# A hybrid streaming encoder step on one core: wider memsets between GpSimd operations, and late attention probabilities scaled by whichever of two engines the planner picks

## The chip, the core and the metric

The kernel runs on one core of a Trainium2 chip. A core has a matrix engine (PE in the profile; its weight loads are listed apart as PEld), a vector engine (DVE), a scalar engine (ACT), a general engine called GpSimd (POOL), and a queue (SP) from which this kernel issues its transfers between the chip's memory and the core's own memory. Each engine works through its instructions in the order in which they were written; semaphores make one engine wait for another.

The metric is the time of one execution in device microseconds. Before the change, three executions took 1264.11, 1261.85 and 1261.01 us, a median of 1261.85 us.

## The reference

One layer of a streaming encoder is computed for a prompt of 2048 frames and a sample of 64 frames, with 1024 features. Half of the mixed features come from an attention of 8 heads by 64 over a band of 576 keys (512 earlier frames and the chunk of 64 that the query is in), the other half from a gated linear recurrence of 4 heads by 128. Both share one input projection from 1024 to 4096 columns.

```python
def mixer_layer(x, ln_g, w_in, lb, norm_g, w_out, attn_fn, s0):
    aq, ak, av, ag, hq, hf, hi, hg = jnp.split(rms_norm(x, ln_g) @ w_in, SPLITS, axis=-1)
    o_a = attn_fn(heads(aq), k, v).reshape(B, T, W_A) * jax.nn.silu(ag)
    o_b, S = hgrn2_branch(hq, hf, hi, hg, lb, norm_g, s0)
    y = x + jnp.concatenate([o_a, o_b], axis=-1) @ w_out
    return y, k, v, S

def band_attention(q, k, v, rel, valid, rel_bias):
    s = jnp.einsum('bnqhd,bnkhd->bnhqk', q, k) * ATTN_SCALE + bias
    s = jnp.where(valid[None, :, None], s, NEG_INF)
    p = jax.nn.softmax(s, axis=-1)
    return jnp.einsum('bnhqk,bnkhd->bnqhd', p, v)
```

A last RMSNorm follows the layer. The outputs are the normalized rows, the newest keys and values, and the states of the recurrence. All inputs are float32.

## The kernel before

**Precision and tiling.** Float32 operands are split into a high and a low part, and a product is made of three matmuls (high by high, low by high, high by low). The prompt is worked in four superblocks of 512 frames; the 64 frames of the sample ride along with the second. For each superblock, 32 projections of 128 columns are made in a fixed list (`JOBS`): for each of four groups, the four parts of the recurrence (`hf`, `hq`, `hi`, `hg`) and the four of the attention (`pg`, `pq`, `pk`, `pv`). As soon as a group is projected, its recurrence or its pair of attention heads is worked beside the projections that follow. The tiles `xh` and `xl` are the two parts of the normalized input, `w` the weights, `acc` the banks of results; in the attention `s` holds scores, `pr` probabilities, `nm` the negated row maxima, `sm` the row sums, `tr` transposed probabilities, `ph` their two parts, `pv` the product with the values, and `mixa` the gated result. In the recurrence, `pf`, `sf`, `fq` and `fk` are small decay factors made on GpSimd from `eb`; with them `q` and `k` are scaled before `g`, `bl`, `asb` and so on are formed.

**What sets the order.** No order is written out by hand. A planner (class `Plan`, line 53) runs a main generator, which issues the projections' matmuls two at a time, and many small generators ("threads") for everything else, and it keeps a clock for every engine. Each operation passes through `Queue.__getattr__`, so nearly all rows of the profile carry its line, 266. There the operation's estimated cost is charged to its engine's clock; a thread that has asked for an engine goes on when the estimated time has come. An estimate that changes therefore changes which thread goes next, and with it the order of the operations from there on, on every engine. `Plan.pick` returns the engine whose clock, plus a cost given with the call, is the lowest.

**The breath.** When three or more GpSimd operations are issued while GpSimd's clock is ahead of the matrix engine's, the planner puts a memset of a small tile, `C.breath`, between them. The planner charges a memset on GpSimd 95 ns and 0.85 ns for each column.

**The softmax.** For 128 query rows of one head, one vector instruction adds the bias to the scores and leaves the row maximum (`pr<-s,bias`, shown as ISA in the order and as CUSTOM_DVE_ANT_0 in the profile); ScalarE takes the exponential and the row sum (`pr<-pr,nm`); VectorE takes the reciprocal of the sum (`RECIPROCAL sm`); then the row is multiplied with it (`pr<-pr,sm`). This last step, in `softmax_exp`, runs on VectorE. It runs on ScalarE once the set `have` contains `"parts"`, which the program adds when the output projection has begun to run beside the attention. That is so only for the last pair of heads of the last superblock: 8 of the 128 x 640 scalings, out of 96.

**The output projection.** `w_out` is split on the chip by the thread `out_weights` during the third superblock and written to memory (`wod<-xn`, 28 transfers); the input rows of the next superblock are loaded to `xn` tiles (`xn<-in_x_prompt_dram`), whose sum of squares (`ck<-xn`) and root (`rstd`) ScalarE computes before VectorE scales them and the matrix engine transposes them (`g<-ident,xn`). Near the end of the program the output projection adds partial sums in `xn<-xn,acc` on VectorE, after ScalarE has copied one of the banks (`asb<-acc`).

Of the kernel before, what the change touches and what calls it, by code (L numbers as in the profile page):

```python
# [8 lines left out]
F32 = mybir.dt.float32  # L9
# [8 lines left out]
P = 128  # L18
D = 1024
# [353 lines left out]
def hymba_step(  # L373
# [24 lines left out]
    C = Plan()  # L398
# [6 lines left out]
    cst = ctx.enter_context(tc.tile_pool(name="cst", bufs=1))  # L405
# [7 lines left out]
    def T(pool_, shape, dt, tag, **kw):  # L413
        uid[0] += 1
        C.name(homes.get(id(pool_), ""), tag, kw.get("bufs") or 1, f"{tag}_{uid[0]}")
        return pool_.tile(list(shape), dt, tag=tag, name=f"{tag}_{uid[0]}", **kw)
# [37 lines left out]
    mask = T(cst, [P, P], U32, "mask")  # L454
    eps_t = T(cst, [P, 1], F32, "eps")
    one_t = T(cst, [P, 1], F32, "one")
    C.breath = T(cst, [P, 1], F32, "breath")
    reset = T(cst, [P, 512], F32, "reset")
    asb = [T(cst, [P, 4, P], F32, f"asb{i}") for i in range(2)]
    g_norm = T(cst, [P, NHB], F32, "gnorm")  # L460
# [5 lines left out]
    have = set()  # L466
# [544 lines left out]
    def softmax_rows(d, h, qc, spans, bcol, nk, out):  # L1011

        yield lambda: d.q_n >= qc + P and d.k_n >= qc + P and d.bias_at is not None
        yield max(d.q_t, d.k_t, d.bias_at) + 300.0
        yield from tk["s_ps"].get()
        yield from tk["pr"].get()
        sps = s_ps()
        for part in (d.q, ql):
            for i, (k0, kn) in enumerate(spans):
                mm(sps[:, i, :kn], part[:, h, qc : qc + P], d.kd[:, h, k0 : k0 + kn], kn,  # L1020
                   start=part is d.q, stop=part is ql)
        t = C.pe()
        yield "D", t
        s = T(wk, [P, 640], F32, "pr", bufs=PRB)
        nm = T(wk, [P, 2], F32, "nm", bufs=4)
        ns, kn = len(spans), spans[0][1]
        dve.tensor_tensor_reduce(
            s[:, :nk].rearrange("p (a c) -> p a c", a=ns), sps[:, :ns, :kn],
            d.bias[:, h, bcol : bcol + nk].rearrange("p (a c) -> p a c", a=ns),
            1.0, 3e38, ALU.add, ALU.min, nm[:, 0:1])  # L1030
        t = C.dve(nk + 80, t)
        tk["s_ps"].put(1, t)
        d.left -= 1
        if d.left == 0:
            if d.sb == len(SUPER) - 1 and d.p == NPAIR - 1:
                have.add("scores")
                tk["x4"].put()
            tk["bias"].put()
        yield "A", t
        yield from softmax_exp(s, nm, nk, out, t)  # L1040

    def softmax_exp(s, nm, nk, out, t):
        sm = T(wk, [P, 1], F32, "sm", bufs=4)
        act.activation(s[:, :nk], s[:, :nk], AF.Exp, bias=nm[:, 0:1], scale=-1.0, accum_out=sm)
        t = C.act(nk + 300, t)
        yield "D", t
        dve.reciprocal(sm, sm)
        t = C.dve()
        if "parts" in have:
            yield "A", t  # L1050
            act.activation(s[:, :nk], s[:, :nk], AF.Copy, scale=sm)
            t = C.act()
        else:
            dve.tensor_scalar(s[:, :nk], s[:, :nk], sm, None, ALU.mult)
            t = C.dve()
        out.append((s, t))
# [184 lines left out]
    def sample_a(d, c0, marks):  # L1241
# [41 lines left out]
        yield "A", t  # L1283
        out = []
        yield from softmax_exp(s, nm, 576, out, t)
        pr, t = out[0]
        yield lambda: marks[-1]["pv"] and turn["ph"] == turn["given"]
# [1008 lines left out]
```

## Time and profile before

| what | value |
|---|---|
| median of three executions | 1261.85 us |
| the profiled execution | 1260.86 us, 0.99 us below that median |
| its span, first to last instruction | 1259.0 us |
| matrix engine busy | 1238.8 us of it (98%) |
| VectorE, ScalarE, GpSimd busy | 891.9, 706.9 and 379.9 us |
| breath memsets | 36, of one column each |
| scalings of 640 columns on VectorE / on ScalarE | 88 / 8 |

A row of a timeline gives the start, the duration, the engine, the operation with what it writes and reads, its size, how many like it stand together, and in brackets how long the engine had been idle and what ended that idle time. Durations overlap, since an engine begins its next instruction before the last one's results are written; a matrix engine that issues at its full pace starts a matmul of 512 columns every 0.23 us (1.40 us for six of them).

### The profile page before, as it was taken

What the parts mean: (1) busy time and instruction counts of PE and PEld (TensorE: products, weight loads), DVE (VectorE), ACT (ScalarE), POOL (GpSimd) and SP (SyncE); (2) the same over time, 40 slices, a digit from 0 to 9 for tenths busy, and PEclk for the clock granted to TensorE, in tenths of its full rate; (3) what the DMA queues carried; (4) which work ended last, traced back from release to release, by engine and by line L of the source; (5) the groups of instructions that cost most, each with busy time, mean ns of one, the idle gap of its engine ahead of it and who ended that gap; (6) DMA issues with size and microseconds to landing.
All of it is one profiled execution on the core that took longest, in us unless ns stands there. A gap on an engine that the chain in (4) does not pass through costs nothing. (4 is left out here: it accounts for less than half of the span.)

```text
span 1259.0 us, 22201 instructions
## 1 busy us (share of the span) xinstructions
PE 1238.8 (98%) x8120; PEld 1081.6 (86%) x8120; DVE 891.9 (71%) x1854; ACT 706.9 (56%) x1548; POOL 379.9 (30%) x703
## 2 busy tenths in 40 slices
PE   9999999999999999999999999999999999999997
PEld 8788887999999999998888888998888888788786
DVE  7786968766857678686584849783838574578886
ACT  6453546665656557575565656764636454753443
POOL 7766655111120210202533634110101104451110
PEclk9999999999999999999999999999999999999999
DMA  7887787645354554636879597646454657886331
GB/s 288 301 288 244 247 282 281 219 168 202 138 188 142 181 200 144 216 125 236 272 248 303 206 364 254 220 164 210 144 212 136 222 178 279 324 277 203 126 134 67
DMA packets 94830, 271.72 MB, mean 216 GB/s; under 512 B 10305, under 2 KB 43073, under 8 KB 77058
## 3 DMA queue, kind: packets, MB, share of 16 engines
q1 hardware_dynamic: 94722, 270.31, 61.4%
q8 instruction: 64, 1.05, 0.3%
q14 instruction: 44, 0.36, 0.1%
HBM read 186.66 MB, written 83.62 MB: 215 GB/s over the span
## 5 line engine op out<-in xcount | busy, mean ns | idle before, releaser
L266 PE MATMUL acc<-xh,w 128*128 128x512 f32 (+2 forms) x2720 | 568.4, 348 | 1.0 <-ACT sig L266 0.8
L266 PEld LDWEIGHTS acc<-xh,w 128*128 128x128 f32 x2720 | 436.7, 189 | 51.7 <-issue 1.4
L266 PE MATMUL acc<-xl,w 128*128 128x512 f32 (+2 forms) x1360 | 297.4, 348 | 0.0
L266 PEld LDWEIGHTS acc<-xl,w 128*128 128x128 f32 x1360 | 219.3, 189 | 24.9 <-issue 0.5
L266 POOL TENSOR_TENSOR mixa<-mixa,sga 128x256 f32<-128x256 f32 (+1 forms) x36 | 29.8, 828 | 334.8 <-DVE mixa L266 259.6
L266 DVE CUSTOM_DVE_ANT_0 pr<-s,bias 128x640 f32<-128x640 f32 (+5 forms) x144 | 100.7, 703 | 34.5 <-PE s L266 33.9
L266 ACT ACTIVATE pr<-pr,nm 128x640 f32<-128x640 f32 (+4 forms) x132 | 100.7, 763 | 39.0 <-DVE nm L266 37.9
L266 ACT CAST ph<-tr 128x512 fp32r<-128x512 f32 (+3 forms) x176 | 88.1, 507 | 59.7 <-PE tr L266 27.9
L266 POOL TENSOR_TENSOR w<-wraw,w 128x256 fp32r<-128x256 f32 x120 | 105.3, 906 | 46.9 <-DVE w L266 25.9
L266 DVE TENSOR_TENSOR ph<-tr,ph 128x512 fp32r<-128x512 f32 (+3 forms) x176 | 101.1, 589 | 10.0 <-ACT ph L266 8.8
L266 PE MATMUL pv<-ph,v 128*128 128x256 f32 (+2 forms) x344 | 97.2, 373 | 3.1 <-DVE ph L266 2.4
L266 PE MATMUL tr<-ident,pr 128*128 128x128 f32 x580 | 91.2, 273 | 2.4 <-DVE pr L266 1.2
L266 PEld LDWEIGHTS tr<-ident,pr 128*128 128x128 f32 x580 | 70.4, 140 | 16.6 <-issue 3.8
L266 ACT ACTIVATE sig<-acc 128x256 f32<-128x256 f32 (+2 forms) x86 | 42.7, 497 | 73.6 <-PE acc L266 73.3
L266 ACT COPY vT<-acc 128x512 f32<-128x512 f32 (+2 forms) x64 | 31.3, 488 | 71.2 <-PE acc L266 71.1
L266 DVE TENSOR_SCALAR pr<-pr,sm 128x640 f32<-128x640 f32 (+3 forms) x124 | 67.9, 547 | 4.4
L266 DVE TENSOR_TENSOR mixa<-mixa,pv 64x256 f32<-64x256 f32 (+1 forms) x144 | 56.8, 394 | 18.9 <-ACT mixa L266 14.7
L266 PEld LDWEIGHTS pv<-ph,v 128*128 128x128 f32 x344 | 57.4, 190 | 10.3 <-issue 2.0
L266 ACT ACTIVATE sig<-sig 128x512 f32<-128x512 f32 (+2 forms) x109 | 57.3, 528 | 10.0 <-DVE gk L266 7.3
L266 PE MATMUL s<-kd,q 128*128 128x320 f32 (+3 forms) x232 | 56.9, 315 | 0.2
L266 POOL TENSOR_TENSOR xn<-wraw,xn 128x256 fp32r<-128x256 f32 x48 | 37.8, 803 | 62.2 <-ACT xn L266 62.1
L266 PE MATMUL s<-kd,ql 128*128 128x320 f32 (+3 forms) x232 | 55.6, 309 | 0.0
(319 smaller groups left out, 2064.5 us busy)
## 6 DMA issues: line engine op xcount, KB each, us to landing
w<-wd SPq DMA_DIRECT2D x96, 1024.0 KB, 5.1
wd<-w SPq DMA_DIRECT2D x32, 1024.0 KB, 7.6
wraw<-in_w_in_dram SPq DMA_DIRECT2D x30, 512.0 KB, 5.5
wod<-xn SPq DMA_DIRECT2D x28, 512.0 KB, 5.0
xn<-in_x_prompt_dram SPq DMA_DIRECT2D x23, 512.0 KB, 5.5
bias<-biasd SPq DMA_DIRECT2D x12, 640.0 KB, 7.5
carry<-kd SPq DMA_DIRECT2D x12, 512.0 KB, 8.0
carry<-v SPq DMA_DIRECT2D x12, 512.0 KB, 5.2
```

The source lines that it names most:

```text
L266: r = f(*args, **kw)
```

## The change

The breath tile has 128 columns rather than one, so each of its memsets writes 128, and the planner charges it 204 ns rather than 96. And a late scaling goes to ScalarE only where the planner's clocks say so: VectorE is chosen if its clock plus 680 ns is not above ScalarE's plus 780 ns (or the current time, or the time at which the reciprocal is done, where these are later than a clock).

```diff
@@ -454,7 +454,7 @@
     eps_t = T(cst, [P, 1], F32, "eps")
     one_t = T(cst, [P, 1], F32, "one")
-    C.breath = T(cst, [P, 1], F32, "breath")
+    C.breath = T(cst, [P, P], F32, "breath")
     reset = T(cst, [P, 512], F32, "reset")
@@ -1046,7 +1046,7 @@
         dve.reciprocal(sm, sm)
         t = C.dve()
-        if "parts" in have:
+        if "parts" in have and C.pick(t, D=680.0, A=780.0) == "A":
             yield "A", t
             act.activation(s[:, :nk], s[:, :nk], AF.Copy, scale=sm)
             t = C.act()
```

In the built program the choice falls on VectorE all 8 times: VectorE has 96 scalings of 640 columns, ScalarE none. There are 35 breaths. Apart from these and a few sums that move between GpSimd and VectorE, the instructions are the same, and their order, with the tiles' running numbers left out, is the same except at four stretches: in the first tens of microseconds, around 715 us, between the third and the fourth superblock (around 764 to 860 us), and in the last pair's attention (around 1069 to 1110 us).

The first place is on the matrix engine, in the first recurrence of the program. `acc` rows are projections, `g<-q,k` the recurrence's small products, `g<-ident,bl` a transpose that needs VectorE's `bl`. Before:

```order
L266 MATMUL acc_600<-xh_156,w_433 128x512 x8
L266 MATMUL acc_600<-xl_157,w_433 128x512 x2
L266 MATMUL g_624<-q_135_518,k_136_519 32x32
...
L266 MATMUL acc_600<-xl_157,w_433 128x512 x6
L266 MATMUL acc_600<-xh_156,w_433 128x512 x2
L266 MATMUL g_672<-ident_69,bl_619 128x128 x4
L266 MATMUL acc_600<-xh_156,w_433 128x512 x6
```

After:

```order
L266 MATMUL acc_596<-xh_156,w_433 128x512 x8
L266 MATMUL acc_596<-xl_157,w_433 128x512 x4
L266 MATMUL g_625<-q_136_526,k_137_527 32x32
...
L266 MATMUL acc_596<-xl_157,w_433 128x512 x4
L266 MATMUL acc_596<-xh_156,w_433 128x512 x6
L266 MATMUL g_676<-ident_69,bl_618 128x128 x4
L266 MATMUL acc_596<-xh_156,w_433 128x512 x2
```

Two more projection matmuls stand ahead of the small products, and four more ahead of the transposes.

The second place is SP's queue of transfers between the third and the fourth superblock. `wod` rows write split output weights, `w` rows load projection weights, `xn` rows load input rows of the fourth superblock, `kd`, `v` and `bias` are for the next pair of heads. Before:

```order
L266 DMA wod_69_141<-xn_9280 256x1x512
L266 DMA wod_73_145<-xn_9279 256x1x512
L266 DMA w_9812<-wd_46_118 128x2048
L266 DMA xn_9836<-in_x_prompt_dram 128x1024
L266 DMA xn_9839<-in_x_prompt_dram 128x1024
L266 DMA mixd_17_89<-mixa_9657 128x256
L266 DMA kd_9905<-carry_3_26_98 128x2x512
L266 DMA v_9906<-carry_3_26_98 128x1024
L266 DMA bias_9910<-biasd_34_106 128x1280
L266 DMA w_9921<-wd_55_127 128x2048
```

After:

```order
L266 DMA wod_69_141<-xn_9303 256x1x512
L266 DMA kd_9833<-carry_3_26_98 128x2x512
L266 DMA v_9834<-carry_3_26_98 128x1024
L266 DMA bias_9838<-biasd_34_106 128x1280
L266 DMA mixd_17_89<-mixa_9653 128x256
L266 DMA wod_73_145<-xn_9302 256x1x512
L266 DMA w_9903<-wd_55_127 128x2048
L266 DMA xn_9940<-in_x_prompt_dram 128x1024
L266 DMA xn_9943<-in_x_prompt_dram 128x1024
L266 DMA w_9955<-wd_51_123 128x2048
```

The two loads of input rows now stand behind the last write of output weights and behind the write of `mixa`, and `kd`, `v` and `bias` stand ahead of both.

The third place is VectorE in the last pair's attention, where the late scalings are. Before:

```order
L266 RECIPROCAL sm_12863<-sm_12863 128x1
L266 ISA pr_12873,nm_12874<-s_12865,bias_12688 128x640
L266 ISA nm_12874 128x1
L266 RECIPROCAL sm_12885<-sm_12885 128x1
L266 ISA pr_12903,nm_12904<-s_12887,bias_12688 128x640
L266 ISA nm_12904 128x1
L266 TENSOR_TENSOR v_12684<-tr_12897,v_12684 128x4x128
L266 COPY sig_12913<-tr_12897 128x512
L266 RECIPROCAL sm_12917<-sm_12917 128x1
L266 ISA pr_12932,nm_12933<-s_12919,bias_12688 128x640
L266 ISA nm_12933 128x1
L266 TENSOR_TENSOR xn_12215<-xn_12215,acc_12880 128x512
```

There the subtractions `ph` (two rows of `ph<-tr,ph`) follow the last of these rows. After:

```order
L266 RECIPROCAL sm_12862<-sm_12862 128x1
L266 TENSOR_SCALAR pr_12855<-pr_12855,sm_12862 128x640
L266 ISA pr_12873,nm_12874<-s_12864,bias_12686 128x640
L266 ISA nm_12874 128x1
L266 RECIPROCAL sm_12896<-sm_12896 128x1
L266 TENSOR_SCALAR pr_12873<-pr_12873,sm_12896 128x640
L266 TENSOR_TENSOR v_12682<-tr_12891,v_12682 128x4x128
L266 COPY sig_12909<-tr_12891 128x512
L266 ISA pr_12919,nm_12920<-s_12898,bias_12686 128x640
L266 ISA nm_12920 128x1
L266 TENSOR_TENSOR ph_12925<-tr_12914,ph_12925 128x512
L266 TENSOR_TENSOR xn_12213<-xn_12213,acc_12879 128x512
```

The scalings stand behind their reciprocals on VectorE, and the first subtraction `ph` stands ahead of the sum `xn<-xn,acc` rather than behind it.

## The prediction

> **What bounds the kernel now.** I read the page's busy times first, then busy time by stretches of the span, then the list of what the matrix engine waits for, then the chain that ended last, and the timeline around each place where the order changes.
>
> ```profile
> PE 1238.8 (98%) x8120; PEld 1081.6 (86%) x8120; DVE 891.9 (71%) x1854; ACT 706.9 (56%) x1548; POOL 379.9 (30%) x703
> ```
>
> The matrix engine (PE) is busy for 1238.8 of 1259.0 us. Neither edit touches the number of projections, so only its 20.2 idle microseconds can shrink, or grow. Where they lie is seen by stretches; the columns are start and end, length, and busy time with the count for PE, its weight loads, VectorE, ScalarE and GpSimd, then the granted clock, the share of the transfer engines and GB/s.
>
> ```profile
> 0.00:80.00 80.00, 75.38 (x471) 63.73 (x472) 60.09 (x112) 41.98 (x89) 55.33 (x92) 1.00 0.83 303
> 760.00:830.00 70.00, 69.39 (x506) 61.14 (x505) 58.75 (x114) 49.67 (x110) 15.27 (x29) 1.00 0.60 215
> 1069.00:1109.00 40.00, 37.63 (x199) 31.35 (x198) 23.20 (x54) 27.91 (x56) 21.32 (x38) 1.00 0.80 293
> 1240.00:1259.00 19.00, 12.44 (x54) 9.73 (x52) 9.56 (x16) 3.80 (x12) 0.00 (x0) 0.92 0.19 72
> ```
>
> Of the 20.2 us, 4.6 lie in the first 80 us, 6.6 in the last 19 us, which the change leaves in order, 0.6 at the boundary between the third and fourth superblock, and 2.4 in the last pair's attention. What can be won is thus 4.6 + 0.6 + 2.4 = 7.6 us at most, 0.6% of the time. The list of waits (engine and instruction, what it waited for, total, times, longest) names the pieces:
>
> ```profile
> PE pv L266 <- DVE ph L266: 2.4, 2, 1.4
> PE g L266 <- POOL one L266: 1.4, 1, 1.4
> PE g L266 <- DVE xl L266: 1.2, 5, 0.4
> PE g L266 <- DVE asb L266: 1.0, 1, 1.0
> PE g L266 <- DVE k L266: 0.8, 2, 0.5
> ```
>
> The two waits for `ph` are in the last pair's attention, those for `asb` and the longest for `k` in the first recurrence. GpSimd is named once, before any breath is written, so breaths reach PE only through VectorE. Of the chain that ended last I show one row: a run of 119 projection matmuls that start together after the last pair's result has gone through memory; before them PE was idle for about 0.2 us, so that an earlier end of the attention moves the rest with it.
>
> ```profile
> 1132.69 27.88 PE acc L266 x119
> ```
>
> **The first recurrence: a gain of 0.7 us.**
>
> ```profile
> 36.88 0.10 POOL L266 MEMSET breath<- 128x1 f32 x1
> 38.66 0.19 POOL L266 COPY fk<-eb 128x4 f32<-128x4 f32 x1
> 39.22 0.79 DVE L266 TENSOR_TENSOR k<-k,fk 128x256 f32<-128x256 f32 x1
> 40.07 1.01 PE L266 MATMUL g<-q,k 128*32 128x64 f32 x52 [0.53 <-DVE k L266]
> 42.51 0.62 PE L266 MATMUL acc<-xh,w 128*128 128x512 f32 x2
> 44.12 0.63 PE L266 MATMUL g<-ident,bl 128*128 128x128 f32 x4 [0.99 <-DVE asb L266]
> ```
>
> GpSimd makes the factors one after another, with three breaths among them; `k<-k,fk` on VectorE waits for the last, and PE for that: 0.53 us. The transposes of `bl` come late too. Two matmuls begun at 42.51 at 0.23 us each would have let them start at 42.97; they started at 44.12, so 1.15 us were lost. The order now puts two more projection matmuls ahead of the small products and four ahead of the transposes, 4 x 0.23 = 0.93 us of work done in time that PE waited. Against it stand two wider memsets ahead of `fk` (the third now follows it). A 128-column memset is in the trace once, beside the group of the breaths (minimum, median, maximum in ns):
>
> ```profile
> 0.80 0.20 POOL masks.py:197 MEMSET ident<- 128x128 f32 x1 [0.29 <-POOLq L2283]
> L266 POOL MEMSET breath<- x36: 88/98/642, 23.0 to 1112.7; 128x1 f32 x36
> ```
>
> Each wider breath costs 0.20 - 0.10 = 0.10 us, two cost 0.2, and since the chain from GpSimd over VectorE to PE has no slack here, they count in full: -0.93 + 0.2 = -0.7 us. The bounds are -1.7 (both waits gone, 0.53 + 1.15) and +0.4 (the memsets lengthen the chain twice over and the next product waits as long as before).
>
> **Breaths elsewhere: 0.2 us lost.** The other 33 cost 33 x 0.10 = 3.3 us of GpSimd, which is busy for 30% of the span. They are hidden by PE's projections, as nothing in PE's list waits on GpSimd there. I take 0.2 us, for the few that stand in a chain to VectorE. The bounds are 0 and 3.3, the latter if all such cover were gone; the low end is the nearer, because PE has under 8 us of waits anywhere outside the tail.
>
> **The boundary to the fourth superblock: 0.5 us lost.**
>
> ```profile
> 788.70 1.06 ACT L266 ACTIVATE ck<-xn 128x1024 bf16<-128x1024 f32 x1
> 790.21 0.20 ACT L266 ACTIVATE rstd<-rstd 128x1 f32<-128x1 f32 x1
> 792.42 0.33 SPq L266 DMA_DIRECT2D mixd<-mixa  x1
> 794.28 3.66 SPq L266 DMA_DIRECT2D w<-wd  x2
> 801.36 0.83 ACT L266 CAST kd<-vT 64x256 fp32r<-64x256 f32 x2
> 803.84 0.37 ACT L266 COPY vT<-acc 128x256 f32<-128x256 f32 x1 [1.64 <-PE acc L266]
> 805.64 0.66 PE L266 MATMUL g<-ident,xn 128*128 128x128 f32 x4 [0.16 <-DVE xl L266]
> 820.39 0.66 PE L266 MATMUL g<-ident,xn 128*128 128x128 f32 x4 [0.38 <-DVE xl L266]
> xn<-in_x_prompt_dram SPq DMA_DIRECT2D x3, 512.0 KB, 5.8
> w<-wd SPq DMA_DIRECT2D x3, 1024.0 KB, 7.6
> ```
>
> Before, the input rows are on their way at 782 us and ScalarE squares them at 788.70, in time of its own. Now their two loads stand in SP's queue behind the write of `mixa` (792.42), the last write of output weights and a weight load. They are issued at about 794 us and land, by 5.8 us and half a megabyte between them, at about 800 and 801.5. On ScalarE their squares and roots, 1.7 us a tile (788.70 to 790.41), now stand between the `kd` casts, which end at 802.2, and the copy of `vT`, which before started at 803.84 after 1.64 us of idle time. Two tiles make 3.4 us, so that copy and the casts of `xh` behind it come at about 805.6, 1.8 us later; PE's own work there is also placed about 0.8 us later (eight more matmuls of 256 columns or scores ahead of the transposes), which leaves it waiting for about 1.0 us. What goes is the waits of the two PE rows, 0.16 + 0.38 = 0.54 us: together +0.5. The bounds are -0.5 (the square of the first tile fits into idle time before the casts) and +6.0 (the rival below).
>
> **The last pair: a gain of 1.4 us.**
>
> ```profile
> 1077.03 2.02 PE L266 MATMUL acc<-w,slot 128*128 128x512 f32 x8
> 1080.02 0.70 PE L266 MATMUL pv<-ph,v 128*128 128x512 f32 x2 [0.96 <-DVE ph L266]
> 1089.58 0.39 PE L266 MATMUL acc<-w,xl 128*128 128x512 f32 x1
> 1091.37 0.48 PE L266 MATMUL pv<-ph,v 128*128 128x256 f32 x2 [1.41 <-DVE ph L266]
> 1078.58 0.69 DVE L266 TENSOR_TENSOR xn<-xn,acc 128x512 f32<-128x512 f32 x1 [1.61 <-ACT asb L266]
> 1090.20 0.69 DVE L266 TENSOR_TENSOR xn<-xn,acc 128x512 f32<-128x512 f32 x1 [2.66 <-ACT asb L266]
> L266 ACT ACTIVATE pr<-pr,sm x8: 813/830/833, 1071.1 to 1100.5; 128x640 f32<-128x640 f32 x8
> L266 DVE TENSOR_SCALAR pr<-pr,sm x124: 286/553/1035, 66.7 to 1037.4; 128x640 f32<-128x640 f32 x88, 128x128 f32<-128x128 f32 x8, 128x256 f32<-128x256 f32 x8, 128x384 f32<-128x384 f32 x8
> ```
>
> Eight matmuls from 1077.03 end their turn at 1078.90, and `pv` started at 1080.02: 1.12 us late. The second `pv` could have started at 1089.81 and started at 1091.37: 1.56 late. Both times VectorE held the subtraction that makes `ph` behind a sum `xn<-xn,acc`, which waited for ScalarE's copy `asb` for 1.61 and 2.66 us; and ScalarE was late because scalings of 0.83 us stood ahead of its casts and copies. Now ScalarE loses 8 x 0.83 = 6.6 us, and the first `ph` stands ahead of the sum, so both waits, 2.68 us, can go. VectorE takes on 8 x 0.553 = 4.4 us in a stretch where it is busy for 23.2 of 40, which leaves room on the whole. But it works in order: each scaling stands ahead of the next instruction that reads scores, or of a `ph`. Going through the new order by hand with the rows' durations, I find six of the eight covered by idle time, and two not: one score bank comes free about 0.4 us late, and one later `ph` about 0.8 us. So -2.68 + 1.2, about -1.4 us. The bounds are -2.9 (no new wait, and the 0.2 before the 119 matmuls go too) and +2.3 (as long a wait for `ph` as before, and the lengthening worked out in the rival below).
>
> **The sum.** -0.7 + 0.2 + 0.5 - 1.4 = -1.4 us. The profiled execution took 1260.86 us, 0.99 below the median of the three, so it would take 1259.5; on the median of 1261.85 I forecast 1260.4 us.
>
> **The rivals.** *All named waits go.* Nothing takes the place of the waits at the redrawn places: 0.53 + 1.15 + 0.54 + 2.68 = 4.9 us, or 1257.0 us. For it speaks that the planner draws the order from its clocks anew and that the new order mends exactly the places that wait. Against it speaks that a work order redrawn at four places seldom leaves no wait behind.
>
> *The input rows come late (slower).* Both loads stand behind a weight load, and the row at 794.28 shows two weight loads held until 797.94, because their tiles were in use. If the first of them waits so long, the input rows are issued 3.7 us later, at about 798; and at the 7.6 us of the stretch's weight loads rather than 5.8, they land 1.8 us later still. ScalarE then stands at their squares with the casts of `xh` behind it, and PE, which needs `xh`, waits as long: 5.5 us more than in the sum, 1265.9 us. It decides once the second tile lands after about 802.5 us, when ScalarE would otherwise reach it. Against it: the hold probably belongs to the second of the two weight loads, which stays behind the input rows.
>
> *VectorE and GpSimd get in each other's way.* The scaling takes 553 ns in the middle and up to 1035, and the long ones stand beside GpSimd's work:
>
> ```profile
> 767.68 1.02 DVE L266 TENSOR_SCALAR pr<-pr,sm 128x640 f32<-128x640 f32 x1
> 1081.99 1.43 POOL L266 TENSOR_TENSOR slot<-sig,slot 128x256 fp32r<-128x256 f32 x2 [18.03 <-ACT slot L266]
> ```
>
> GpSimd idles for 18 us up to 1081.99, so the first scalings run free; about five come after it, and 5 x (1.02 - 0.55) = 2.3 us are added to VectorE there. With half of the other breaths' 3.3 us uncovered as well, the sum becomes -1.4 + 2.3 + 1.7 = +2.6, or 1264.5 us, and over 1265.6 if the waits for `ph` stay. The Trainium skill, "SBUF — State Buffer", section "Who interferes with whom", speaks against the change in the same way: a `tensor_scalar` in its two-port mode and GpSimd lock each other out for a whole instruction, while ScalarE never waits on anyone; the two lengths of the scaling agree with it, and by it the sum would be that of this rival. The same section says that a vector instruction with two inputs in SBUF contends with GpSimd instructions that read SBUF and not with one that only writes it; by it a memset of 0.20 us would be a wider opening for VectorE, which no row of before shows, and the 0.2 us lost to breaths would become a small gain.
>
> *The new condition never picks VectorE* has no chance: the order has all eight scalings there.
>
> **How the numbers follow.** About 0.3% (3.8 us) is what a measurement of this kernel can tell from no change. The sum has a chance of 0.42; its own range, 1258 to 1263, lies within that. All waits gone has 0.27, faster. The late input rows have 0.18, slower. The two engines in each other's way have 0.13, of which 0.06 over 0.3% slower. That makes faster 0.27, same 0.49, slower 0.24. The range runs from 1256.0, a microsecond under the second case, to 1266.5, just over the third; beyond it lie 0.1 on each side.
>
> **What would show it.** In the profile after, the 1.0 and 0.5 us that PE waits for `asb` and `k` early should shrink; the waits of `pv` for `ph` near 1080 and 1091 should be gone, with `xn<-xn,acc` behind `ph`; scalings on VectorE in that stretch should take 0.55 to 1.0 us; and near 805 PE should wait for `xh` or `xl` about 1 us. The prediction is wrong if PE's idle time there is several microseconds (input rows after 803 us), if `pv` still waits over a microsecond for `ph`, or if a wait appears in a stretch whose order did not change.

## The result and the profile after

The changed kernel takes 1254.63 us (median; 1253.5 to 1255.5), the kernel before beside it 1261.53 us. The ratio is 0.9942, with a 95% interval of 0.9929 to 0.9955: 0.58% faster, some 7 us. The prediction was 1260.4 us with a range from 1256.0 to 1266.5, so the time lies below the range.

The page's first lines after (busy time, share of the span and instructions):

```profile
span 1252.0 us, 22191 instructions
PE 1234.3 (99%) x8120; PEld 1081.3 (86%) x8120; DVE 893.8 (71%) x1865; ACT 701.4 (56%) x1540; POOL 376.3 (30%) x696
```

The span is 7.0 us shorter, but PE's idle time fell only from 20.2 to 17.7 us. The other 4.5 us came out of its *busy* time, with the same 8120 matmuls. A sum over idle time alone could not have found them. The stretches after, to be held against those of before:

```profile
0.00:80.00 80.00, 76.27 (x477) 64.48 (x478) 62.99 (x115) 43.54 (x92) 56.35 (x92) 1.00 0.83 304
760.00:830.00 70.00, 70.00 (x518) 63.52 (x517) 55.39 (x110) 49.65 (x112) 21.09 (x38) 1.00 0.63 214
1069.00:1109.00 40.00, 39.51 (x209) 33.27 (x208) 30.15 (x68) 23.17 (x52) 24.00 (x40) 1.00 0.94 337
```

PE is busier in all three. To see where the span was saved, I matched the matmuls of the two traces one by one and took the difference of their start times (after less before) at eight marks; what a stretch won or lost is the difference between its two ends. The other columns do the same for three of the kernels below.

| stretch of before, us | after | breath of 128 columns alone | choice of engine alone | unused tile alone |
|---|---|---|---|---|
| 0 to 65 | -1.4 | -1.5 | +1.1 | 0.0 |
| 65 to 238 | +0.4 | +0.4 | +2.5 | +1.2 |
| 238 to 630 | +0.2 | +0.1 | +0.3 | +0.1 |
| 630 to 748 | +1.0 | +0.8 | +0.4 | -0.1 |
| 748 to 890 | -2.1 | -2.2 | 0.0 | -0.1 |
| 890 to 1062 | +0.1 | +0.1 | 0.0 | +0.1 |
| 1062 to 1118 | -2.5 | +0.3 | -1.6 | -0.1 |
| 1118 to the end | -2.6 | -1.9 | -0.3 | -1.9 |
| sum | -6.9 | -3.9 | +2.4 | -0.7 |

Such a column compares one execution with one. In the first 240 us kernels with the same order differ by more than 2 us among themselves, so the sums are not the kernels' times, which are medians of several executions. From 240 us up to the last pair, kernels of the same order agree within 0.5 us in every stretch, and there the columns can be read; in the last two stretches they differ by up to 1.1 us, in the last pair because of one scaling on VectorE that comes up below.

Of the four stretches that won over a microsecond, three had a term in the forecast, which missed in size or, at the boundary, in sign; the last, 2.6 us in the output projection at the end, was not forecast at all. Most of it is a change of *pace*, the time from the start of one matmul to the start of the next. The chain of waits has there, in both kernels, an unbroken run of 180 matmuls of 512 columns (start, duration, engine, tile). Before, and then after:

```profile
1210.68 41.77 PE acc L266 x180
```

```profile
1204.52 40.93 PE acc L266 x180
```

180 of them take 0.84 us less: 0.2321 us each before, 0.2274 after, at the same granted clock (1.00 in both stretches). Nothing waits in either run.

The cause I looked for is where the tiles lie. A tile of 128 columns takes 512 bytes in each partition where one of a single column took 32, so every tile that is allocated behind the breath moves up by 480 bytes: the weights and inputs, `q`, `kd`, `v` and `ph`. The `slot` tiles of the output projection come from a pool that is filled from the other end, and stay. In the built programs, 410 matmuls of the last stretch have their two operands at addresses that differ by 224 modulo 256 bytes before; after, by 0.

### The profile page after: what moved, and what is told of

It is laid out like the page before. It is cut to its first block, busy times and chain, and to the rows that moved or that the text cites. A ratio compares the mean times of both kernels' runs of the same rounds, so it can differ in the third digit from the quotient of the medians.

```text
span 1252.0 us, 22191 instructions
## 1 busy us (share of the span) xinstructions
PE 1234.3 (99%) x8120; PEld 1081.3 (86%) x8120; DVE 893.8 (71%) x1865; ACT 701.4 (56%) x1540; POOL 376.3 (30%) x696
## 4 chain that ended last, share of the span: by engine, by line
PE 82%; POOL 5%; DVE 4%; DMA 3%; issue 3%; ACT 2%; SPq 0%; DVEq 0%; POOLq 0%; ACTq 0%
PE acc L266 60%; PE g L266 6%; PE tr L266 6%; PE s L266 5%; PE pv L266 5%; POOL w L266 3%; DMA wd<-w 1%; POOL pf L266 1%; DVE xn L266 1%; DMA xn<-in_x_prompt_dram 1%; DMA wod<-xn 1%; DMA lbg<-in_lb_gamma_dram 1%; DVE pr L266 1%; SPq L266 0%; POOL wraw L266 0%
## 5 line engine op out<-in xcount | busy, mean ns | idle before, releaser
L266 DVE TENSOR_SCALAR pr<-pr,sm 128x640 f32<-128x640 f32 (+4 forms) x132 | 71.9, 545 | 4.7
```

The source lines that it names most:

```text
L266: r = f(*args, **kw)
```

## Experiments

Twelve kernels were run. All ratios are to the kernel before.

**An unused tile of 120 columns**, allocated behind the one-column breath. It moves the tiles as the change does and leaves the order of all instructions as before.

```diff
     C.breath = T(cst, [P, 1], F32, "breath")
+    T(cst, [P, P - 8], F32, "rest_of_breath")
```

> The kernel before, with a tile of 120 columns that nothing uses set behind the breath's one column, so that every later tile of the core's own memory moves by 480 bytes, to the places of the kernel after; the order of all instructions is that of before. Theory 1 (places: a matmul of 512 columns takes 0.227 us where its two operands' addresses differ by a multiple of 64 bytes and 0.233 us where they do not, and the slots of the output projection are such a case before): about 470 matmuls of the last 190 us start 0.006 us closer together, 1258.8 us, 2.7 under before. Theory 2 (order: the last stretch is shorter because of what the redrawn attention hands on): no change, 1261.5 us.

Measured: 1260.65 us, ratio 0.9992 (0.9983 to 1.0000). The run of 180 has the pace of after:

```profile
1210.71 40.93 PE acc L266 x180
```

The last stretch gets 1.9 us shorter by the trace, with not one instruction moved, so for these 1.9 us the handing-on by the attention is refuted. PE's busy time falls from 1238.8 us by 2.0 us:

```profile
PE 1236.8 (98%) x8120; PEld 1081.3 (86%) x8120; DVE 892.5 (71%) x1854; ACT 707.1 (56%) x1548; POOL 381.7 (30%) x703
```

The time as a whole moved by 1 us only, less than the 2.7 expected; the first 240 us were 1.3 us longer in this execution.

**The slots alone moved by 32 bytes**, through a longer last tile of their pool.

```diff
-        more.append(lambda: T(pw, [P, 512], F32, "rest"))
+        more.append(lambda: T(pw, [P, 520], F32, "rest")[:, :512])
```

> The kernel before, with the last tile of the output projection's own pool made 32 bytes longer, which moves only that pool's tiles, the slots among them, by 32 bytes; same order. Theory 1 (places): slots and weights now differ by a multiple of 64 bytes, so the pace of the last stretch is 0.227 us and the time 1258.8 us, as with all other tiles moved. Theory 2 (order): 1261.5 us. If moving the other tiles matters for another reason (ScalarE, VectorE or transfers at other addresses), this one stays at 1261.5 and the unused tile does not.

Measured: 1261.27 us, ratio 0.9994 (0.9985 to 1.0002); the run of 180:

```profile
1211.52 41.30 PE acc L266 x180
```

0.2294 us each, halfway. Moving the slots alone changes the pace, and so does moving the tiles behind the breath while the slots stay, so it is the distance of the two operands and not some other moved tile. But a distance that is a multiple of 64 bytes (here 192 modulo 256) does not give the full pace: my first rule was wrong.

**Four slots at four distances**, 256, 320, 384 and 448 bytes modulo 512 from the weights (`slot` becomes four tags with 64 bytes between them).

```diff
+        kinds = [0]
...
-            m = T(pw, [P, 2, 4, P], F32R, "slot", bufs=4)
-            return m[:, 0], m[:, 1]
+            kinds[0] += 1
+            i = (kinds[0] - 1) % 4
+            m = T(pw, [P, 1024 + 16 * (i < 3)], F32R, "slot" + "abcd"[i])
+            return [m[:, c : c + 512].rearrange("p (k t) -> p k t", t=P) for c in (0, 512)]
...
-        more.append(lambda: T(pw, [P, 512], F32, "rest"))
+        more.append(lambda: T(pw, [P, 520], F32, "rest")[:, :512])
```

> The kernel before with four slots at four different distances from the weight tiles: 256, 320, 384 and 448 bytes modulo 512 (before, all at 480); same order. If only a multiple of 64 bytes matters, all four run at 0.227 us and the time is 1258.8 us. If a multiple of 128 or 256 is needed, the slots at 320 and 448 (or all but 256) run at 0.231 to 0.233 us, and the time is 1259.8 to 1260.8 us. Theory 2 (order): 1261.5 us.

Measured: 1262.05 us, ratio 0.9998 (0.9989 to 1.0007). Within this one execution the pace follows the distance, slot by slot. I put the trace's start-to-start times of 512-column matmuls beside the addresses in the built programs; pauses over 0.3 us are left out. The distance is the address of the operand that is held less that of the one that is streamed, modulo 256 bytes:

| distance, bytes | median ns from start to start | number | kernel |
|---|---|---|---|
| 0 | 227 | 2390 | after |
| 192 | 229 | 134 | four distances |
| 96 | 232 | 56 | before |
| 128 | 232 | 218 | four distances |
| 64 | 233 | 136 | four distances |
| 32 | 232 (mean 233) | 410 | after, moved by 32 bytes |
| 160 | 234 | 19 | before |
| 224 | 234 | 410 | before |

**The kernel after, moved by 32 bytes**: the breath has 120 columns and is charged as 128, so the order is that of after.

```diff
-    C.breath = T(cst, [P, P], F32, "breath")
+    C.breath = T(cst, [P, P - 8], F32, "breath")
...
-                return 95.0 + 0.85 * n, 60.0, False
+                return 95.0 + 0.85 * (P if n == P - 8 else n), 60.0, False
```

> The kernel after with a breath of 120 columns that is still charged as 128: the order is that of after, and all tiles behind it lie 32 bytes lower, so that slots and weights no longer differ by a multiple of 64 bytes. Theory 1 (places): the last stretch loses its 2.7 us again, 1257.3 us. Theory 2 (order): 1254.6 us.

Measured: 1255.62 us, ratio 0.9953 (0.9939 to 0.9967). The run of 180 has the slow pace again, in the order of after:

```profile
1205.04 41.71 PE acc L266 x180
```

The last stretch won 0.4 us in place of 2.6 by the trace, so about 2.2 us of it are places; the time lost 1.0 us by the medians and 1.4 by the ratios, less than that, with overlapping intervals. So the pace is settled in both directions, the share of it in the time only to between 1 and 2 us.

**The breath of 128 columns alone.**

```diff
-    C.breath = T(cst, [P, 1], F32, "breath")
+    C.breath = T(cst, [P, P], F32, "breath")
```

> The breath of 128 columns alone; late scalings on ScalarE as before. Theory 1 (places) with the order's share elsewhere: early -1.4, 80 to 760 us +0.9, boundary to the fourth superblock -2.1, last pair as before, last stretch -2.7: 1256.2 us. Theory 2 (order alone, the last stretch's gain handed on by the attention): -2.6 without the last stretch, 1258.9 us.

Measured: 1258.69 us, ratio 0.9976 (0.9966 to 0.9986). The table's third column shows what it brings: the early gain, the loss between 630 and 748 us, the boundary, and the pace. The last pair wins nothing. The two waits of `pv` stay (PE's list of waits between 1060 and 1140 us), and by the start times one more `pv` comes 0.4 us late, at 1097.6:

```profile
PE pv L266 <- DVE ph L266: 2.5, 2, 1.5
```

My sum for it (1256.2) was too low by 2.5 us; the time is nearer to the 1258.9 of theory 2, whose reason the unused tile refutes. The stretches of this execution do sum to 3.9 us less, and it was the fastest of its seven.

**The choice of engine alone.**

```diff
-        if "parts" in have:
+        if "parts" in have and C.pick(t, D=680.0, A=780.0) == "A":
```

> The choice of engine alone; breath of one column. Theory 1 (places): the two waits of pv for ph go, -2.4 us in the last pair, and the last stretch keeps its pace of 0.233 us: 1259.1 us. Theory 2 (the attention hands its gain on): the last stretch is 2.7 us shorter too, 1256.4 us. Prediction's own sum for this part: -1.4, 1260.1 us.

Measured: 1260.35 us, ratio 0.9996 (0.9982 to 1.0009), which is not told from no change. The trace shows the mechanism all the same: of the two waits of `pv` for `ph`, 2.4 us together, one of 1.1 us is left, at another place.

```profile
1098.60 1.64 DVE L266 TENSOR_SCALAR pr<-pr,sm 128x640 f32<-128x640 f32 x1
1101.63 0.73 PE L266 MATMUL pv<-ph,v 128*128 128x512 f32 x2 [1.05 <-DVE ph L266]
```

The last pair wins 1.6 us by itself, and 2.5 + 0.3 = 2.8 us where it is added to the wider breath (the column of after against that of the breath alone). The two edits are thus worth more together than apart; by the ratios, 0.24% and 0.04% apart and 0.58% together. Two causes show in the traces. The order drawn by the breath alone has the one wait more in the last pair, which the choice removes too. And the wait left here comes behind a scaling that took 1.64 us on VectorE (the upper row), where it takes 0.61 us with the wider breath; a later experiment comes back to it. They make about 1.0 of the 1.2 us by which the last pair wins more; for the rest of the difference between the times the traces name no cause.

**128 columns written, one charged.** Places of after, order of before.

```diff
+    C.breath = T(cst, [P, P], F32, "breath")
...
+                return 95.0 + 0.85 * (1 if n == P else n), 60.0, False
```

> The breath writes 128 columns but the planner charges one, so the order is that of before and the places those of after. Against the kernel with the unused tile it shows the memsets' own cost: the prediction's 0.2 to 0.4 us more (36 of 0.10 us, mostly hidden), bounds 0 and 3.6 us; a gain, if wider memsets let VectorE in. Expected 1259.0 us by theory 1 (places), 1261.8 by theory 2.

Measured: 1260.59 us, ratio 0.9987 (0.9978 to 0.9997). That is the unused tile's time within the noise, so 36 longer memsets cost nothing that shows.

**One column written, 128 charged**, places of after, scalings as before.

```diff
+    T(cst, [P, P - 8], F32, "rest_of_breath")
...
+                return 95.0 + 0.85 * (P if n == 1 else n), 60.0, False
```

> The breath writes one column, is charged as 128, and an unused tile puts all others at the places of after; scalings as before. Order and places are then those of the width alone without its longer memsets. If the gain of the width is order and places, this equals the width alone to 0.3 us (1256.2 us by theory 1); if the longer memset itself gives VectorE room, this one is slower by that.

Measured: 1258.65 us, ratio 0.9970 (0.9960 to 0.9981), the same as the breath of 128 columns. What the wider breath brings is thus its *charge* in the planner, which redraws the order, and its *size*, which moves the tiles; that it takes longer brings nothing that can be measured while the late scalings are on ScalarE. The opening for VectorE that the prediction read out of the Trainium skill ("SBUF — State Buffer", section "Who interferes with whom") is no gain in the time here.

**The kernel after with a one-column breath charged as 128.**

```diff
+    T(cst, [P, P - 8], F32, "rest_of_breath")
...
+                return 95.0 + 0.85 * (128 if n == 1 else n), 60.0, False
...
+        if "parts" in have and C.pick(t, D=680.0, A=780.0) == "A":
```

> The kernel after, but its breath writes one column and is still charged as 128, with an unused tile that keeps all places: order and places are those of after, only the 35 memsets are 0.10 us shorter. If order and places are the whole of the gain: 1254.6 us, the same as after. If the longer memset itself lets VectorE in: slower than after, by up to 1 us.

Measured: 1253.92 us, ratio 0.9936 (0.9923 to 0.9949), in the time not told from after. One place of the trace is different: the seventh of the eight late scalings took 1.73 us on VectorE, and PE waited for it, through `ph`:

```profile
1090.87 1.73 DVE L266 TENSOR_SCALAR pr<-pr,sm 128x640 f32<-128x640 f32 x1
1090.06 1.47 POOL L266 TENSOR_TENSOR sig<-sig,reset 128x256 f32<-128x256 f32 x2
1091.46 0.76 POOL L266 TENSOR_TENSOR slot<-wraw,slot 128x256 fp32r<-128x256 f32 x1
1092.13 0.12 POOL L266 MEMSET breath<- 128x1 f32 x1
1093.99 0.73 PE L266 MATMUL pv<-ph,v 128*128 128x512 f32 x2 [1.61 <-DVE ph L266]
```

The scaling started while GpSimd worked and ended at 1092.60, 0.47 us after the start of GpSimd's next breath: it had stood until GpSimd came to its next memset. In the kernel after, the same scaling took 0.61 us, and GpSimd's two sums beside it took longer:

```profile
1091.94 1.70 POOL L266 TENSOR_TENSOR sig<-sig,reset 128x256 f32<-128x256 f32 x2
1092.43 0.61 DVE L266 TENSOR_SCALAR pr<-pr,sm 128x640 f32<-128x640 f32 x1
```

The Trainium skill, "SBUF — State Buffer", section "Who interferes with whom", says that a VectorE operation in its two-port mode and GpSimd lock each other out for whole instructions; this row agrees, though the scaling stood through the second sum and the operation behind it and not through one instruction only, and it is the price of the prediction's third rival. It fell on one scaling of eight.

This is no accident of one execution. Five kernels have a breath of one column and their late scalings on VectorE: this one, the next three, and the choice of engine alone. In these the seventh scaling took 1.73, 1.74, 1.73, 1.03 and 1.64 us, and ended 0.45 to 0.47 us after the start of GpSimd's next breath. In the two with a wide breath, after and after with 120 columns, it took 0.61 and 0.55 us. The order of PE's matmuls is the same here as in after, and from 1085 to 1100 us this kernel loses 1.1 us by their start times. So with the scalings on VectorE the longer memset is worth about 1 us at this place, in the trace; an interval of 1.6 us to either side cannot show that in the time. A likely reason, not shown by a run of its own: longer breaths put GpSimd's sums back, so that the scaling starts 0.5 us behind the first of them rather than 0.8 and gets its turn ahead of the second.

**The same, with all operands a multiple of 256 bytes apart**: without the unused tile, the attention's and the projections' pools moved by 128 bytes and the slots by 96.

```diff
     pa = ctx.enter_context(tc.tile_pool(name="pa", bufs=1))
+    T(pa, [P, 32], F32, "shift")
...
-        more.append(lambda: T(pw, [P, 512], F32, "rest"))
+        more.append(lambda: T(pw, [P, 536], F32, "rest")[:, :512])
```

> As the one before it (order of after, breath of one column charged as 128), but without the unused tile, and with the tiles of the attention and the projections moved by 128 bytes and the slots by 96, so that ph and v, ph and the slots, and the slots and all weights lie a multiple of 256 bytes apart. Theory (the pace of a 512-column matmul depends on the distance of its two operands modulo 256 bytes: 0.227 us at 0, 0.229 at 192, 0.231 to 0.232 at 96 and 128, 0.233 and more at 32, 64, 160 and 224): the 162 matmuls that stand at 128 in the kernel after go from 0.231 to 0.227, 0.6 us less, 1254.0 us. If it is not the distance: pace of pv and of ph with slots stays at 0.231.

Measured: 1254.15 us, ratio 0.9935 (0.9923 to 0.9947), the same as the one before. The pace did what was expected: the 162 matmuls that stood at 128 bytes went from a median of 231 ns to 227, and 0.8 us went from 240 us to the end by the trace. That is too little to be told in the time.

**Charges of 64 and of 256 columns**, otherwise as the one-column breath charged as 128.

```diff
-                return 95.0 + 0.85 * (128 if n == 1 else n), 60.0, False
+                return 95.0 + 0.85 * (64 if n == 1 else n), 60.0, False
```

> As the first of this group, with the breath charged as 64 columns: same places as after, another order. If the redrawn order is better because GpSimd is charged more truly (0.20 us), half the charge gives about half of the order's gain outside the last pair (2.4 us of early, boundary and the loss around 650 and 730): about 1255.8 us. If each charge simply draws another order, the waits at those three places are unlike both, and the time lies anywhere from 1253 to 1258 us.

> As the first of this group, with the breath charged as 256 columns (0.31 us). If a truer charge is what helps, too large a charge is worse than 128: about 1255.5 to 1257 us. If each charge draws another order: anywhere from 1253 to 1258 us, with other waits early, around 730 and at the boundary to the fourth superblock.

Measured: 1254.81 us, ratio 0.9942 (0.9929 to 0.9955), and 1255.13 us, ratio 0.9946 (0.9934 to 0.9958). All three charges give the same time within the noise, and each has its own waits: by the start times, the small products and the transposes of the first recurrence come 0.84 and 0.25 us late with 64, 0.25 and 1.15 with 256 (after: 0.39 and 0.71); the boundary wins 2.1 us with 64 and 1.2 with 256. So 128 is no special value. All three orders are better at the boundary than that of a charge of one column. Whether a truer charge is better in general, or the old one was an unlucky draw, these runs do not tell.

## Why the prediction was wrong, step by step

**"Only its 20.2 idle microseconds can shrink".** This step failed first. The same matmuls got quicker, because moving the tiles changed the distance between their operands. The built program showed that a tile that grows by 480 bytes stands ahead of others, and I priced it as time on GpSimd alone. It is worth 1.9 to 2.2 us by the traces. The Trainium skill calls the matrix engine's two reads independent ("SBUF — State Buffer", section "Who interferes with whom"); the measured dependence on the distance of their addresses does not fit that word as it stands, and the measurement decides.

The step failed on a second ground. Places took 2.0 of the 4.5 us out of PE's busy time; the other 2.5, by subtraction, are delays that the page counts as busy. The row of a matmul of 512 columns lasts 0.39 us where one starts every 0.23, so 0.16 us of each delay is hidden: the transposes that were 1.15 us late have 0.99 us of idle time. A delay under 0.16 us shows as no idle time at all. The 7.6 us were therefore no upper bound.

**The first recurrence, -0.7.** Right in kind. The two waits fell from 0.53 and 0.99 us to

```profile
39.98 1.01 PE L266 MATMUL g<-q,k 128*32 128x64 f32 x52 [0.20 <-DVE k L266]
44.05 0.63 PE L266 MATMUL g<-ident,bl 128*128 128x128 f32 x4 [0.54 <-DVE asb L266]
```

and a third, ahead of `g<-asb,gi`, went, 0.31 us by the start times. The stretch won 1.4 us. I had charged two longer memsets in full (0.2), but `fk` came no later than before (38.52 against 38.66 us), and I had given the third wait nothing.

**Breaths elsewhere, 0.2 lost.** The memsets themselves cost nothing that shows, though one reason I gave for that was wrong: PE's idle time outside the last 19 us was 20.2 - 6.6 = 13.6 us, not under 8. What was lost, 1.0 us between 630 and 748 us, is order: I had named a redrawn stretch near 715 us and given it no term. Near 730 us ScalarE waited until a transfer had written split output weights out of an `xn` tile that it was to fill anew; behind that stood its copy `ob`, GpSimd's `k` (728.86 us, before the change 727.52) and VectorE's `q`, and PE waited for `q`:

```profile
726.99 0.71 ACT L266 CAST xn<-wraw 128x256 fp32r<-128x256 f32 x2 [4.88 <-DMA wod<-xn]
728.86 1.05 POOL L266 TENSOR_TENSOR k<-ob 128x512 f32<-128x512 f32 x1
730.69 0.50 PE L266 MATMUL g<-q,ones 128*128 128x512 f32 x1 [0.37 <-DVE q L266]
```

**The boundary, +0.5.** The sign was wrong: it won 2.1 us. The rows after show which assumption failed.

```profile
786.33 0.32 SPq L266 DMA_DIRECT2D mixd<-mixa  x1
791.91 4.68 SPq L266 DMA_DIRECT2D xn<-in_x_prompt_dram  x2
801.59 1.06 ACT L266 ACTIVATE ck<-xn 128x1024 bf16<-128x1024 f32 x1
803.20 1.04 ACT L266 ACTIVATE ck<-xn 128x1024 bf16<-128x1024 f32 x1
804.81 0.35 ACT L266 COPY vT<-acc 128x256 f32<-128x256 f32 x1
805.06 0.59 ACT L266 CAST xh<-g 128x512 fp32r<-128x512 f32 x1
804.38 1.19 PE L266 MATMUL acc<-xh,w 128*128 128x256 f32 x8
```

ScalarE's part came out in kind: the two squares stand behind the `kd` casts and the copy of `vT` starts at 804.81 rather than 803.84, 1.0 us later where I had 1.8. But PE did not wait for the casts behind it. It has eight matmuls of 256 columns ready at 804.38, while the first cast of `xh` starts only at 805.06, so those eight do not read what is being cast. I had put their wait down at 1.0 us without looking at which part of `xh` they read. And the waits that went were more than the 0.54 us I counted: the start times of before show delays over 0.1 us at 770, 771, 789, 805, 807, 817 and 820 us, some 1.7 us together, and hardly any of them after. PE's list of waits names only 0.5 us of it. Which change of the order removed each of them was not tried apart. The rival of late input rows did not come about: the loads were issued at 791.9 and held, but landed in 4.5 us (median of three), and PE did not wait for them.

**The last pair, -1.4.** Right in mechanism. Both waits went, `ph` stands ahead of the sum, and one new wait came, of 0.66 us by the start times rather than the 1.2 I allowed:

```profile
1074.51 0.69 DVE L266 TENSOR_TENSOR ph<-tr,ph 128x512 fp32r<-128x512 f32 x1
1075.11 0.68 DVE L266 TENSOR_TENSOR xn<-xn,acc 128x512 f32<-128x512 f32 x1
1075.79 0.71 PE L266 MATMUL pv<-ph,v 128*128 128x512 f32 x2
1094.44 0.73 PE L266 MATMUL pv<-ph,v 128*128 128x512 f32 x2 [0.49 <-DVE ph L266]
1095.42 0.81 DVE L266 TENSOR_SCALAR pr<-pr,sm 128x640 f32<-128x640 f32 x1
```

Six of the eight late scalings took 0.55 to 0.56 us, one 0.61 and one 0.81, so VectorE lost 0.3 us to GpSimd and not the 2.3 of the third rival. The 0.24 us ahead of the long run at 1132 went as well, which I had kept for the bound. (My own figures, -2.68 and +1.2, make -1.5; the sum has -1.4.) What the third rival priced, the choice alone and the breath of one column do show, on one scaling; the wider breath avoids it here, and I had not seen that the two edits are linked in this way.

**The case I gave 0.27** (all named waits go, 1257.0 us) was nearest, 2.4 us too long. Its waits went nearly as it said; it lacked the pace and most of what the boundary won, and the loss between 630 and 748 us, which it also lacked, offset a part of that.

## What to carry to other kernels

When a change alters the size of a tile, list which tiles move in the core's memory before pricing it: the time of a matmul can depend on where its operands lie relative to each other, and a page that calls the engine busy does not show it, while the start-to-start time of a long unbroken run does. A planner whose costs set the order turns any change of a cost into a change of order at places far away; the waits that go and come there are read from the start times of matched instructions, since the list of waits names only part of them. An interval of 0.13% to either side cannot show a gain of 1 us in 1250; such a gain is looked for in the rows of one place, in several kernels. And of a wait that a new order might bring, look up what the waiting instruction reads before giving it a price.

## What was not expected of the hardware

A matmul of 512 columns of split float32 starts every 227 ns where its two operands' addresses differ by a multiple of 256 bytes, and every 229 to 234 ns at the seven other distances, all multiples of 32 bytes; over 180 of them that is 40.93 against 41.77 us. Moving the slots alone changes the pace (41.30 us), and in the order of after, moving the weights by 32 bytes brings the slow one back (41.71 us), so it is the distance that counts. What in the chip makes it so is not shown here, nor whether matmuls of 256 or 320 columns have it, since nearly all of those stood at distance 0.

A scaling on VectorE that takes 0.55 us by itself took 1.03 to 1.74 us beside GpSimd's sums in five kernels, and each time ended 0.45 to 0.47 us after the start of the next small memset on GpSimd. The memsets in question had one column and took 0.09 to 0.12 us.
